# RMSNorm with ReLU on one core: 32-row blocks, joined stores, and VectorE's last two chunks taken whole

## The chip, the cores and the metric

One Trainium2 chip, one of its cores. The metric is the device time of one execution in microseconds.

## The reference, cut to what matters

```python
x = np.random.randn(16, 1024, 512).astype(np.float32)     # 16,384 rows of 512
gamma = np.ones(512, dtype=np.float32)
rms = np.sqrt(np.mean(x ** 2, axis=-1, keepdims=True) + 1e-5)
return np.maximum(x / rms * gamma, 0).astype(np.float32)
```

33.55 MB come in and 33.55 MB go out. Each row needs one sum of squares, one scale, one product with gamma and a maximum with 0.

## The kernel before

A partition owns 16 consecutive rows of each of 8 chunks, so a chunk is 4.19 MB and a packet of a transfer 32 KB. The kernel keeps six chunks in SBUF at a time. ScalarE sums the squares of 8 rows (a "group") and takes the roots; VectorE scales the group. SyncE issues all transfers and waits for two marks in VectorE's loop, `tick3` and `tick1`, before it lets stores go.

```python
xv = x2.rearrange("(c p k) d -> c p k d", p=P, k=K)       # K = 16
ov = out2.rearrange("(c p k) d -> c p k d", p=P, k=K)
# ... loads of chunks 0 to 5 are issued first (cut) ...
nc.sync.wait_ge(tick3, 6)
store(0)
store(1)
for s in range(2):
    nc.sync.wait_ge(sem_slot[s], 32)
    load(7 + s)                                           # chunks 6 and 7
nc.sync.wait_ge(tick1, 11)
for i in range(2, nchunks):
    store(i)
# ... (cut) ...
with nc.vector.Fori(0, ngroups) as gi:                    # 16 groups
    take(nc.vector, sq, 1)                                # wait and subtract
    # base, col, blk: addresses from gi (cut)
    nc.vector.reciprocal(out=rstd[...], in_=rms[...]).then_inc(sv, 1)
    take(nc.vector, sv, 1)
    for j in range(G):
        r = nc.vector.scalar_tensor_tensor(               # row * rstd * gamma
            out=row, in0=row, scalar=rstd[...], in1=gamma_sb, ...)
        # j == 0: tick1, j == 2: tick3, j == 7: sv
    take(nc.vector, sv, 1)
    nc.vector.tensor_scalar_max(out=blk, in0=blk, scalar1=0.0).then_inc(done, 1)
```

Of the kernel before, what the change touches and what calls it, by code (L numbers as in the profile page):

```python
# [1 line left out]

# [4 lines left out]

F32 = mybir.dt.float32
ALU = mybir.AluOpType
ACTF = mybir.ActivationFunctionType  # L10


@with_exitstack
def kernel(
    ctx: ExitStack,
    tc: tile.TileContext,
    x: bass.AP,
    gamma: bass.AP,
    eps: bass.AP,
    out: bass.AP,  # L20
):




    nc = tc.nc
    P = nc.NUM_PARTITIONS

    x2 = x.flatten_outer_dims()
    out2 = out.flatten_outer_dims()  # L30
    n, d = x2.shape
    rows = n // P
    inv_d = 1.0 / d
    K = 16
    G = 8
    nchunks = rows // K
    nslots = 6
    ngroups = rows // G
    per = K // G
    xv = x2.rearrange("(c p k) d -> c p k d", p=P, k=K)  # L40
    ov = out2.rearrange("(c p k) d -> c p k d", p=P, k=K)

    def sbuf(name, shape):
        return nc.alloc_sbuf_tensor(name, shape, F32).ap()

    gseed = sbuf("gseed", [P, d])
    gamma_sb = sbuf("gamma_sb", [P, d])
    eps_sb = sbuf("eps_sb", [P, 1])
    ss = sbuf("ss", [P, rows])
    rms = sbuf("rms", [P, rows])  # L50
    rstd = sbuf("rstd", [P, rows])
    slots = sbuf("slots", [P, nslots * K * d])
    junk = nc.alloc_psum_tensor("junk", [P, G, d], F32).ap()


    loads = [(0, 0, G), (0, G, K - G)] + [(i, 0, K) for i in range(1, nchunks)]


    sem_half = nc.alloc_semaphore("half")
    sem_slot = [nc.alloc_semaphore(f"slot{s}") for s in range(nslots)]  # L60
    sem_g = nc.alloc_semaphore("gam")
    sem_z = nc.alloc_semaphore("zero")
    ready = nc.alloc_semaphore("ready")
    sq = nc.alloc_semaphore("sq")
    tick1 = nc.alloc_semaphore("tick1")
    tick3 = nc.alloc_semaphore("tick3")
    done = nc.alloc_semaphore("done")
    sa = nc.alloc_semaphore("sa")
    sv = nc.alloc_semaphore("sv")

    def slot_ap(i):
        s = (i % nslots) * K * d
        return slots[:, s:s + K * d].rearrange("p (k d) -> p k d", d=d)

    def load(m):
        i, a, r = loads[m]
        return nc.sync.dma_start(out=slot_ap(i)[:, a:a + r, :],
                                 in_=xv[i][:, a:a + r, :]
                                 ).then_inc(sem_half if m == 0 else sem_slot[i % nslots], 16)

    def take(engine, sem, n):
        engine.wait_ge(sem, n)
        engine.sem_inc(sem, -n)  # L83

    def store(i):
        nc.sync.wait_ge(done, per * (i + 1))
        nc.sync.dma_start(out=ov[i], in_=slot_ap(i)).then_inc(sem_slot[i % nslots], 16)



    ctx.enter_context(tc.manual_schedule(engines={mybir.EngineType.SP}))
    early = 2
    for m in range(early):
        t = load(m)
        tc.no_tile_sem_insts.add(t.ins.name)
    ctx.close()
    tc.close()
    tc.compile()  # L98

    for m, (i, a, r) in enumerate(loads):  # L100
        if m >= early and i < nslots:
            load(m)


    nc.sync.wait_ge(tick3, 6)
    store(0)
    store(1)
    for s in range(2):
        nc.sync.wait_ge(sem_slot[s], 32)
        load(7 + s)  # L110
    nc.sync.wait_ge(tick1, 11)
    for i in range(2, nchunks):
        store(i)

    for m, (i, a, r) in enumerate(loads):
        if m == 0:
            take(nc.gpsimd, sem_half, 16)
        else:
            nc.gpsimd.wait_ge(sem_slot[i % nslots], 32 * (i // nslots) + 16)
        nc.gpsimd.sem_inc(ready, r // G)  # L120

    nc.vector.memset(gseed, 0.0).then_inc(sem_z, 1)  # L122
    nc.vector.memset(eps_sb, eps).then_inc(sem_z, 1)  # L123

    nc.scalar.wait_ge(sem_z, 1)
    nc.scalar.dma_start(out=gseed[0:P:32, :],
                        in_=gamma[None, :].to_broadcast([P // 32, d])
                        ).then_inc(sem_g, 16)
    nc.scalar.preload_act_table(ACTF.Sqrt)  # L129
    take(nc.scalar, sem_z, 2)  # L130
    with nc.scalar.Fori(0, ngroups) as gi:
        take(nc.scalar, ready, 1)
        base = nc.scalar.snap((gi % (nslots * per)) * (G * d))
        col = nc.scalar.snap(gi * G)
        for j in range(G):
            a = nc.scalar.activation(  # L136
                out=junk[:, j, :], in_=slots[:, bass.ds(base + j * d, d)],
                func=ACTF.Square, accum_out=ss[:, bass.ds(col + j, 1)])
            if j == G - 1:
                a.then_inc(sa, 1)  # L140
        take(nc.scalar, sa, 1)
        nc.scalar.activation(out=rms[:, bass.ds(col, G)], in_=ss[:, bass.ds(col, G)],  # L142
                             func=ACTF.Sqrt, bias=eps_sb, scale=inv_d).then_inc(sq, 1)

    take(nc.vector, sem_g, 16)
    nc.vector.stream_shuffle(gamma_sb, gseed, [0] * 32)  # L146
    with nc.vector.Fori(0, ngroups) as gi:
        take(nc.vector, sq, 1)
        base = nc.vector.snap((gi % (nslots * per)) * (G * d))
        col = nc.vector.snap(gi * G)  # L150
        blk = slots[:, bass.ds(base, G * d)]
        nc.vector.reciprocal(out=rstd[:, bass.ds(col, G)],  # L152
                             in_=rms[:, bass.ds(col, G)]).then_inc(sv, 1)
        take(nc.vector, sv, 1)
        for j in range(G):
            row = slots[:, bass.ds(base + j * d, d)]
            r = nc.vector.scalar_tensor_tensor(  # L157
                out=row, in0=row, scalar=rstd[:, bass.ds(col + j, 1)], in1=gamma_sb,
                op0=ALU.mult, op1=ALU.mult)
            if j == 0:  # L160
                r.then_inc(tick1, 1)
            if j == 2:
                r.then_inc(tick3, 1)
            if j == G - 1:
                r.then_inc(sv, 1)
        take(nc.vector, sv, 1)
        nc.vector.tensor_scalar_max(out=blk, in0=blk, scalar1=0.0).then_inc(done, 1)  # L167

    take(nc.sync, done, ngroups)
    take(nc.sync, tick1, ngroups)  # L170
    take(nc.sync, tick3, ngroups)
    for i in range(nchunks - nslots, nchunks):
        take(nc.sync, sem_slot[i % nslots], 32 * (i // nslots + 1))


# [1 line left out]
_INS = ['x', 'gamma', 'eps']  # L177
_OUTS = [((16, 1024, 512), 'float32')]

_NUMBERS = {'eps': 9.999999747378752e-06}  # L180


# [26 lines left out]
```

## Time and profile before

| | before |
|---|---|
| median of 3 runs (range) | 160.52 us (160.39 to 160.58) |
| span of the profiled run | 159.3 us |
| queue 1's share of the 16 DMA engines | 98.2% |
| VectorE busy, last instruction ends at | 126.0 us, 146.4 us |
| last store issued, landed (first to last of the 16 DMA engines) | 146.48, 157.66 to 158.74 us |

The rows of the page by group of instructions (line, engine, operation, operands, shape and count; then busy time and mean ns of one; then the idle time ahead of them and what ended it):

```profile
L157 DVE SCALAR_TENSOR_TENSOR slots<-slots,rstd,gamma_sb 128x512 f32 x128 | 86.2, 747 | 4.8 <-DVEq L83 4.8
L167 DVE TENSOR_SCALAR slots<-slots x16 | 36.7, 2294 | 2.4 <-DVEq L83 0.2
```

The 4.8 us of idle time ahead of 16 first products are 0.30 us each: a semaphore instruction and register work lie between the reciprocal and the product.

Besides the page I use the trace's records of single DMA packets. Each transfer ends, on each of the 16 DMA engines, in a 4-byte packet that puts up its semaphore; the times of these sixteen packets say when each engine is done with it. "First" and "last engine" below are the earliest and the latest of the sixteen.

### The profile page before, as it was taken

The page shows a single profiled execution, that of the slowest core. Times are in us where ns is not written, and L with a number is a line of the kernel's source. Part 1 is how long each engine was busy: PE and PEld are TensorE (multiplying, and loading weights), DVE is VectorE, ACT ScalarE, POOL GpSimd, SP SyncE. Part 2 cuts the span into 40 slices and gives each one's busy share as a digit, 9 for nine tenths or more (in the row PEclk, how much of TensorE's full clock was granted, in tenths as well). Part 3 has the DMA queues.
Part 4 walks back from the last instruction along what each step waited for, and adds up shares of the span by engine and source line. Part 5 has one row for each costly group of instructions (what it writes and reads, how often), then busy time and mean ns, then how long its engine had stood idle before and what let it go on. Part 6 is the DMA issues. An engine that isn't in the chain of part 4 may idle for free. (4 is left out here: it accounts for less than half of the span.)

```text
span 159.3 us, 999 instructions
## 1 busy us (share of the span) xinstructions
DVE 126.0 (79%) x164; ACT 86.3 (54%) x273; POOL 0.2 (0%) x4
## 2 busy tenths in 40 slices
DVE  1012989898999999999999999999999989897000
ACT  0388929889989988988920098898500000000000
POOL 0000000000000000000000000000000000000000
DMA  6999999999999999999999999999999999999995
GB/s 193 405 453 424 502 395 395 502 420 395 453 469 395 395 502 420 395 428 494 395 395 444 461 411 395 486 436 395 453 453 403 411 494 411 403 461 453 395 420 247
DMA packets 2456, 67.12 MB, mean 421 GB/s; under 512 B 276, under 2 KB 276, under 8 KB 280
## 3 DMA queue, kind: packets, MB, share of 16 engines
q1 hardware_dynamic: 2448, 67.11, 98.2%
q10 hardware_dynamic: 8, 0.01, 0.0%
HBM read 33.56 MB, written 33.55 MB: 421 GB/s over the span
## 5 line engine op out<-in xcount | busy, mean ns | idle before, releaser
L157 DVE SCALAR_TENSOR_TENSOR slots<-slots,rstd,gamma_sb 128x512 f32 x128 | 86.2, 747 | 4.8 <-DVEq L83 4.8
L136 ACT ACTIVATE junk<-slots 128x512 f32 x128 | 74.4, 581 | 20.6 <-ACTq L83 20.3
L167 DVE TENSOR_SCALAR slots<-slots x16 | 36.7, 2294 | 2.4 <-DVEq L83 0.2
L136 ACT ACTIVATION_READ_ACCUMULATOR junk<-slots x128 | 23.9, 187 | 0.0
L152 DVE RECIPROCAL rstd<-rms x16 | 3.1, 197 | 5.3 <-DVEq L83 5.3
L142 ACT ACTIVATE rms<-ss,eps_sb x16 | 4.8, 301 | 3.0 <-ACTq L83 3.0
L146 DVE LOAD_MASK_SELECT gamma_sb<-gseed x1 | 0.0, 14 | 5.4 <-DVEq L83 5.4
L129 ACT ACT_TABLE_LOAD x1 | 1.3, 1283 | 4.2 <-issue 4.2
L122 DVE MEMSET gseed<- 128x512 f32 x1 | 0.5, 485 | 2.6 <-PEq L98 2.6
L146 DVE STREAM_SHUFFLE gamma_sb<-gseed 128x512 f32<-128x512 f32 x1 | 0.7, 723 | 0.0
L190 POOL MEMSET const-bfloat16-1.0<- 128x1 bf16 x1 | 0.1, 102 | 0.0
L190 POOL MEMSET const-uint8-127<- 128x1 uint8 x1 | 0.1, 102 | 0.0
L190 POOL MEMSET const-float32-0.0<- 128x1 f32 x1 | 0.1, 99 | 0.2 <-issue 0.2
L190 POOL MEMSET const-float32-1.0<- 128x1 f32 x1 | 0.1, 99 | 0.0
L123 DVE MEMSET eps_sb<- 128x1 f32 x1 | 0.1, 59 | 0.0
## 6 DMA issues: line engine op xcount, KB each, us to landing
out_dram<-slots SPq DMA_DIRECT2D x8, 4096.0 KB, 20.6
slots<-in_x_dram SPq DMA_DIRECT2D x7, 4096.0 KB, 29.7
slots<-in_x_dram SPq DMA_DIRECT2D x2, 2048.0 KB, 9.7
gseed<-in_gamma_dram ACTq DMA_DIRECT2D x1, 8.0 KB
```

The source lines that it names most:

```text
L122: nc.vector.memset(gseed, 0.0).then_inc(sem_z, 1)
L123: nc.vector.memset(eps_sb, eps).then_inc(sem_z, 1)
L129: nc.scalar.preload_act_table(ACTF.Sqrt)
L136: a = nc.scalar.activation(out=junk[:, j, :], in_=slots[:, bass.ds(base + j * d, d)], func=ACTF.Square, accum_out=ss[:, bass.ds(col + j, 1)])
L142: nc.scalar.activation(out=rms[:, bass.ds(col, G)], in_=ss[:, bass.ds(col, G)], func=ACTF.Sqrt, bias=eps_sb, scale=inv_d).then_inc(sq, 1)
L146: nc.vector.stream_shuffle(gamma_sb, gseed, [0] * 32)
L152: nc.vector.reciprocal(out=rstd[:, bass.ds(col, G)], in_=rms[:, bass.ds(col, G)]).then_inc(sv, 1)
L157: r = nc.vector.scalar_tensor_tensor(out=row, in0=row, scalar=rstd[:, bass.ds(col + j, 1)], in1=gamma_sb, op0=ALU.mult, op1=ALU.mult)
L167: nc.vector.tensor_scalar_max(out=blk, in0=blk, scalar1=0.0).then_inc(done, 1)
L190: nc = _bacc.Bacc("TRN2", target_bir_lowering=False, num_devices=1)
```

## The change

The intent: fewer and larger store packets, fewer waits in VectorE's loop, and marks adapted to that.

1. In DRAM a partition owns 32 consecutive rows of chunks 2 and 3, and of 4 and 5. They are still loaded 16 rows at a time but leave in two joined stores with 64 KB packets.
2. Waits no longer subtract; the subtractions come at the end of the loop's body, and addresses are made before the wait.
3. One mark, on the sixth product, in place of two.
4. VectorE loops over 12 groups. Chunks 6 and 7 are taken whole, in two passes of 128 x 8192 each, the second one a custom operation (product and clamp).
5. The two small memsets move to GpSimd.

The core of the diff, with cuts marked:

```diff
+    order = [(L, 0, G), (L, G, G)] + [(L, i * K, K) for i in range(1, nslots)] + [
+        (S, 0, K), (S, K, K), (L, room, K), (L, room + K, K),
+        (S, 2 * K, 2 * K), (S, 4 * K, 2 * K), (S, room, K), (S, room + K, K)]
+    blocks = [(0, K), (K, K), (2 * K, 2 * K), (4 * K, 2 * K), (room, K), (room + K, K)]
 ... (cut)
+            if order[m - 1][0] == L:
+                nc.sync.wait_ge(tick, 6 if a == 0 else 11)
+            nc.sync.wait_ge(done, (a + r) // G)
 ... (cut)
-    with nc.vector.Fori(0, ngroups) as gi:
-        take(nc.vector, sq, 1)
+    with nc.vector.Fori(0, ndyn) as gi:          # ndyn = 12
 ... (cut)
-        take(nc.vector, sv, 1)
+        nc.vector.wait_ge(sv, 1)
         for j in range(G):
 ... (cut)
-            if j == 0:
-                r.then_inc(tick1, 1)
-            if j == 2:
-                r.then_inc(tick3, 1)
+            if j == G - 3:
+                r.then_inc(tick, 1)
 ... (cut)
+    for i in range(nslots, nchunks):
 ... (cut)
+        nc.vector.tensor_tensor(out=blk, in0=blk, in1=fac[:, :, None].to_broadcast([P, K, d]),
+                                op=ALU.mult).then_inc(sv, 1)
+        nc.vector.wait_ge(sv, steps + 2)
+        nc.vector._custom_dve(
+            dve_ops.TENSOR_MUL_SAT, out=blk, in0=blk,
+            in1=gamma_sb[:, None, :].to_broadcast([P, K, d]),
+            s0=float("inf"), s1=0.0).then_inc(done, per)
```

More of the change, by code (lines that the diff above doesn't have):

```diff
@@ L4 @@
 import concourse.tile as tile
-from concourse import bass_utils, mybir
+from concourse import bass_utils, dve_ops, mybir
 from concourse._compat import with_exitstack
@@ L39 @@
     per = K // G
-    xv = x2.rearrange("(c p k) d -> c p k d", p=P, k=K)
-    ov = out2.rearrange("(c p k) d -> c p k d", p=P, k=K)
     def sbuf(name, shape):
@@ L53 @@
     junk = nc.alloc_psum_tensor("junk", [P, G, d], F32).ap()
-    loads = [(0, 0, G), (0, G, K - G)] + [(i, 0, K) for i in range(1, nchunks)]
-    sem_half = nc.alloc_semaphore("half")
-    sem_slot = [nc.alloc_semaphore(f"slot{s}") for s in range(nslots)]
+    L, S = 0, 1
+    room = nslots * K
+    order = [(L, 0, G), (L, G, G)] + [(L, i * K, K) for i in range(1, nslots)] + [
+        (S, 0, K), (S, K, K), (L, room, K), (L, room + K, K),
+        (S, 2 * K, 2 * K), (S, 4 * K, 2 * K), (S, room, K), (S, room + K, K)]
+    blocks = [(0, K), (K, K), (2 * K, 2 * K), (4 * K, 2 * K), (room, K), (room + K, K)]
+    sems = [nc.alloc_semaphore(f"t{m}") for m in range(len(order))]
     sem_g = nc.alloc_semaphore("gam")
@@ L64 @@
     sq = nc.alloc_semaphore("sq")
-    tick1 = nc.alloc_semaphore("tick1")
-    tick3 = nc.alloc_semaphore("tick3")
+    tick = nc.alloc_semaphore("tick")
     done = nc.alloc_semaphore("done")
@@ L69, with here, transfer @@
     sv = nc.alloc_semaphore("sv")
-    def slot_ap(i):
-        s = (i % nslots) * K * d
-        return slots[:, s:s + K * d].rearrange("p (k d) -> p k d", d=d)
-    def load(m):
-        i, a, r = loads[m]
-        return nc.sync.dma_start(out=slot_ap(i)[:, a:a + r, :],
-                                 in_=xv[i][:, a:a + r, :]
-                                 ).then_inc(sem_half if m == 0 else sem_slot[i % nslots], 16)
+    def here(a, r):
+        a %= room
+        return slots[:, a * d:(a + r) * d].rearrange("p (k d) -> p k d", d=d)
+    def transfer(m):
+        kind, a, r = order[m]
+        first, k = max(b for b in blocks if b[0] <= a)
+        there = (out2 if kind == S else x2)[first * P:(first + k) * P].rearrange(
+            "(p k) d -> p k d", k=k)[:, a - first:a - first + r, :]
+        ends = (there, here(a, r)) if kind == S else (here(a, r), there)
+        return nc.sync.dma_start(out=ends[0], in_=ends[1]).then_inc(sems[m], 16)
     def take(engine, sem, n):
@@ L83, in take @@
         engine.sem_inc(sem, -n)
-    def store(i):
-        nc.sync.wait_ge(done, per * (i + 1))
-        nc.sync.dma_start(out=ov[i], in_=slot_ap(i)).then_inc(sem_slot[i % nslots], 16)
     ctx.enter_context(tc.manual_schedule(engines={mybir.EngineType.SP}))
@@ L93 @@
     for m in range(early):
-        t = load(m)
+        t = transfer(m)
         tc.no_tile_sem_insts.add(t.ins.name)
@@ L98 @@
     tc.compile()
-    for m, (i, a, r) in enumerate(loads):
-        if m >= early and i < nslots:
-            load(m)
-    nc.sync.wait_ge(tick3, 6)
-    store(0)
-    store(1)
-    for s in range(2):
-        nc.sync.wait_ge(sem_slot[s], 32)
-        load(7 + s)
-    nc.sync.wait_ge(tick1, 11)
-    for i in range(2, nchunks):
-        store(i)
-    for m, (i, a, r) in enumerate(loads):
-        if m == 0:
-            take(nc.gpsimd, sem_half, 16)
-        else:
-            nc.gpsimd.wait_ge(sem_slot[i % nslots], 32 * (i // nslots) + 16)
-        nc.gpsimd.sem_inc(ready, r // G)
-    nc.vector.memset(gseed, 0.0).then_inc(sem_z, 1)
-    nc.vector.memset(eps_sb, eps).then_inc(sem_z, 1)
+    for m, (kind, a, r) in enumerate(order):
+        if m < early:
+            continue
+        if kind == S:
+            if order[m - 1][0] == L:
+                nc.sync.wait_ge(tick, 6 if a == 0 else 11)
+            nc.sync.wait_ge(done, (a + r) // G)
+        elif a >= room:
+            take(nc.sync, sems[order.index((S, a - room, r))], 16)
+        transfer(m)
+    nc.gpsimd.memset(gseed, 0.0).then_inc(sem_z, 1)
+    nc.gpsimd.memset(eps_sb, eps).then_inc(sem_z, 1)
+    for m, (kind, a, r) in enumerate(order):
+        if kind == L:
+            take(nc.gpsimd, sems[m], 16)
+            nc.gpsimd.sem_inc(ready, r // G)
     nc.scalar.wait_ge(sem_z, 1)
@@ L131 @@
     with nc.scalar.Fori(0, ngroups) as gi:
-        take(nc.scalar, ready, 1)
         base = nc.scalar.snap((gi % (nslots * per)) * (G * d))
         col = nc.scalar.snap(gi * G)
+        nc.scalar.wait_ge(ready, 1)
         for j in range(G):
@@ L138 @@
                 func=ACTF.Square, accum_out=ss[:, bass.ds(col + j, 1)])
-            if j == G - 1:
-                a.then_inc(sa, 1)
-        take(nc.scalar, sa, 1)
+        a.then_inc(sa, 1)
+        nc.scalar.wait_ge(sa, 1)
         nc.scalar.activation(out=rms[:, bass.ds(col, G)], in_=ss[:, bass.ds(col, G)],
                              func=ACTF.Sqrt, bias=eps_sb, scale=inv_d).then_inc(sq, 1)
-    take(nc.vector, sem_g, 16)
+        nc.scalar.sem_inc(sa, -1)
+        nc.scalar.sem_inc(ready, -1)
+    nc.vector.wait_ge(sem_g, 16)
     nc.vector.stream_shuffle(gamma_sb, gseed, [0] * 32)
-    with nc.vector.Fori(0, ngroups) as gi:
-        take(nc.vector, sq, 1)
-        base = nc.vector.snap((gi % (nslots * per)) * (G * d))
+    ndyn = nslots * per
+    with nc.vector.Fori(0, ndyn) as gi:
+        base = nc.vector.snap(gi * (G * d))
         col = nc.vector.snap(gi * G)
         blk = slots[:, bass.ds(base, G * d)]
+        nc.vector.wait_ge(sq, 1)
         nc.vector.reciprocal(out=rstd[:, bass.ds(col, G)],
                              in_=rms[:, bass.ds(col, G)]).then_inc(sv, 1)
-        take(nc.vector, sv, 1)
+        nc.vector.wait_ge(sv, 1)
         for j in range(G):
@@ L159 @@
                 op0=ALU.mult, op1=ALU.mult)
-            if j == 0:
-                r.then_inc(tick1, 1)
-            if j == 2:
-                r.then_inc(tick3, 1)
-            if j == G - 1:
-                r.then_inc(sv, 1)
-        take(nc.vector, sv, 1)
-        nc.vector.tensor_scalar_max(out=blk, in0=blk, scalar1=0.0).then_inc(done, 1)
-    take(nc.sync, done, ngroups)
-    take(nc.sync, tick1, ngroups)
-    take(nc.sync, tick3, ngroups)
-    for i in range(nchunks - nslots, nchunks):
-        take(nc.sync, sem_slot[i % nslots], 32 * (i // nslots + 1))
+            if j == G - 3:
+                r.then_inc(tick, 1)
+        r.then_inc(sv, 1)
+        nc.vector.wait_ge(sv, 2)
+        nc.vector.tensor_scalar_max(out=blk, in0=blk, scalar1=0.0).then_inc(done, 1)
+        nc.vector.sem_inc(sv, -2)
+        nc.vector.sem_inc(sq, -1)
+    steps = 0
+    for i in range(nslots, nchunks):
+        blk = here(i * K, K)
+        fac = rstd[:, i * K:(i + 1) * K]
+        nc.vector.wait_ge(sq, per * (i - nslots + 1))
+        nc.vector.reciprocal(out=fac, in_=rms[:, i * K:(i + 1) * K]).then_inc(sv, 1)
+        nc.vector.wait_ge(sv, steps + 1)
+        nc.vector.tensor_tensor(out=blk, in0=blk, in1=fac[:, :, None].to_broadcast([P, K, d]),
[5 more added lines that the diff above has]
+            s0=float("inf"), s1=0.0).then_inc(done, per)
+        steps += 2
+    take(nc.sync, done, ngroups)
+    take(nc.sync, tick, ndyn)
+    take(nc.sync, sq, ngroups - ndyn)
+    take(nc.sync, sv, steps)
+    take(nc.sync, sem_g, 16)
+    for m, (kind, a, r) in enumerate(order):
+        if kind == S and a + room >= rows:
+            take(nc.sync, sems[m], 16)
 _INS = ['x', 'gamma', 'eps']
```

## The prediction

> **What bounds the kernel now.** The page comes first, its DMA rows before its engine rows.
>
> ```profile
> span 159.3 us, 999 instructions
> DVE 126.0 (79%) x164; ACT 86.3 (54%) x273; POOL 0.2 (0%) x4
> ...
> DMA  6999999999999999999999999999999999999995
> ...
> q1 hardware_dynamic: 2448, 67.11, 98.2%
> ...
> HBM read 33.56 MB, written 33.55 MB: 421 GB/s over the span
> ...
> DVE 1%; issue 0%
> ```
>
> The sixteen DMA engines are busy in every slice but the first and the last; queue 1 alone holds them 98.2% of 159.3, or 156.4 us. VectorE is busy 79% and has done its work before the end. The chain of waits, the last row, names almost nothing: the last instruction ends long before the span, so what ends last is a transfer, which the chain cannot follow. The bound is therefore DMA time plus the idle DMA at both ends.
>
> The second look is the timeline of the queue that issues the transfers, and of VectorE around its release points.
>
> ```profile
> 0.73 4.16 SPq L77 DMA_DIRECT2D slots<-in_x_dram  x7
> 58.30 0.82 SPq L87 DMA_DIRECT2D out_dram<-slots  x2
> 71.23 10.35 SPq L77 DMA_DIRECT2D slots<-in_x_dram  x2
> 98.19 48.62 SPq L87 DMA_DIRECT2D out_dram<-slots  x6
> ```
>
> ```profile
> 96.91 0.20 DVE L152 RECIPROCAL rstd<-rms  x1
> 97.41 5.39 DVE L157 SCALAR_TENSOR_TENSOR slots<-slots,rstd,gamma_sb 128x512 f32 x8 [0.30 <-DVEq L83]
> 102.95 2.29 DVE L167 TENSOR_SCALAR slots<-slots  x1
> ...
> 144.15 2.29 DVE L167 TENSOR_SCALAR slots<-slots  x1
> ```
>
> The first column is the start, the second the length. VectorE's group is eight row products, then one maximum; the reciprocals of two groups are 8.24 us apart. The first store starts at 58.30, exactly as the third row product of the sixth group ends (56.20 + 2 x 0.663 + 0.75 = 58.27); store 2 starts at 98.19, as the first row product of the eleventh group ends (97.41 + 0.75 = 98.16). So VectorE is no bound, but two marks in its loop set when the stores go out.
>
> The records of single DMA packets, third, show how little room the marks leave. Loads 0 to 5 put up their last semaphore packets at 60.68 to 61.05 us, load 7 at 99.57 to 100.08, the last store at 157.66 to 158.74. A transfer issued into an empty queue (the first, issued at 0.73) shows its first packet at 1.75, 1.02 us later. So the first store must be issued by about 59.6 and store 2 by about 98.5 (estimates: landing minus 1.02 us), or the engines run dry. Before, the margins are 1.3 and 0.3 us. The last store is issued at 146.48 for a queue that drains at 147.98: margin 0.5 us.
>
> **What the Trainium skill says.** "DMA: Bandwidth & Descriptors", section "Where 436 GB/s comes from", gives 435.2 GB/s for the ports of one core. The trace agrees: in steady loads 4.194 MB take 9.681 us, or 433 GB/s. At 435.2 the 67.11 MB would take 154.2 us; sixteen times 9.681 is 154.9. So faster packets can give at most 0.7 us altogether, an estimate from that page's figure.
>
> The same page, section "Why small descriptors are slow (HBM only)", tells of a fixed cost of about three cycles per packet. The trace agrees that it is tiny: packets of 16,384 B take 611 ns and of 32,768 B 1,213 ns, so 16 KB cost 602 ns and 9 ns are fixed (less still from one packet's start to the next, about 1,209 ns for 32 KB).
>
> "Perfetto Trace Analysis", section "Per-instruction lifecycle", has a VectorE instruction wait for its semaphores in a hardware queue while the sequencer goes on to decode. Before, every wait in VectorE's loop is a separate semaphore instruction that also subtracts: it runs 0.04 us after the producer ends, takes 21 ns, and the consumer starts only after more decoding. On the issuing queue, where a wait stands alone ahead of a transfer, the records show it inside the transfer's own instruction. I infer, and no run shows yet, that a wait without the subtraction will likewise be folded into the VectorE instruction behind it.
>
> "VectorE: DVE Perf Modes", section "The TRN2 errata", has fp32 tensor_tensor exact at (N + 151) / 0.96 ns. The trace has no such operation; for N = 8,192 the estimate from that page is 8.69 us.
>
> **The change, part by part.**
>
> Descriptors: a partition now owns 32 consecutive rows of chunks 2 to 5. Their loads still take 16 rows at a time, packets of 32 KB with a step of 64 KB. Their stores join in pairs: 4 x 128 = 512 packets of 32 KB become 256 of 64 KB. Per engine 16 packets vanish, of 136. At 5 to 9 ns each that is 0.08 to 0.14 us, plus two semaphore packets of 9 ns. Call it 0.1 us, on the path. The later issue of pairs costs nothing: done counts of 8 and 12 groups are reached at about 80 and 110 us, while their turns come at about 100 and 119.
>
> Waits in VectorE's loop: the gaps are 0.30 us between reciprocal and first row product and 0.16 between last product and maximum. With folded waits I expect them to shrink to about 0.08 and 0.06: 0.22 + 0.10 = 0.32 us a group. The gap ahead of the reciprocal is already hidden under the maximum. ScalarE's first group also starts earlier: 0.32 us lie between its released wait at 8.41 and its first square at 8.73, and 0.18 before the square root; with VectorE's own first wait, about 0.5 us. All this is off the path as long as DMA stays full. It moves the marks.
>
> Marks: both are now the sixth product. Unmoved, it would end at 56.20 + 5 x 0.663 + 0.75 = 60.26 in the sixth group and at 97.41 + 5 x 0.663 + 0.75 = 101.47 in the eleventh. Savings up to there: 0.5 + 6 x 0.22 + 5 x 0.10 = 2.3 us and 0.5 + 11 x 0.22 + 10 x 0.10 = 3.9 us. Issues then fall at 58.0 and 97.6 us, inside 59.6 and 98.5. No hole, no gain. That both results lie so near the old 58.3 and 98.2 speaks for a mark retuned to this faster loop.
>
> Tail of VectorE: twelve groups from about 14.0, at 8.24 - 0.32 = 7.92, end at 109.0. Each of the last chunks is two passes of 8.69 plus a reciprocal of 0.2 and waits of about 0.2: 17.8 us, against 16.5 for two groups before. The end is at 109.0 + 35.6 = 144.6, against 146.44 before. The last store is issued about 144.7, 2.3 us before its limit of 147.0. Store 6 is released at about 127, its turn comes at about 138. So this part is worth 0.
>
> Moving the memsets to GpSimd: gamma is needed at about 14 us, and before it had landed by 7.7. Worth 0.
>
> Sum: 160.52 - 0.1 = 160.4 us.
>
> **The rivals.**
>
> A: waits fold incompletely. Ahead of a row product the trace shows register work of 115 ns between wait and product. If the wait sits on that, only about 0.09 of the 0.30 us goes; store 2 is issued at 101.47 - (0.4 + 11 x 0.09 + 10 x 0.10) = 99.1, and the hole is 0.6 us: 161.0. If the product's wait stays a separate instruction, only the 0.10 is saved: 101.47 - 1.4 = 100.1, a hole of 1.6 us: 162.0. If nothing folds, 101.2 and 60.0 give holes of 2.7 and 0.4: 163.5. For it speaks that register work; against it that the edit puts waits directly ahead of instructions, which would make little sense otherwise, and that the two marks fit the full saving.
>
> B: the custom product-and-clamp runs at half rate. Then a pass takes 17.1 us instead of 8.7, VectorE ends near 161 and the last store near 173. Nothing in this trace shows the operation. Against it: it replaces a multiply and a clamp, an odd thing to do in a tuned kernel at half rate. There are 2.3 us of room, so only a rate below about 0.88 would be felt.
>
> C: the address step of 64 KB, or the larger packet, disturbs the transfers. One per cent on the 33.6 MB concerned is 0.8 us. For it speaks that the packets' durations already vary in stores (up to 1,713 ns). Against it, nearly all stand at 1,213 whatever the direction.
>
> D: the slowest DMA engine gains. The last of the sixteen finishes 1.08 us behind the first and falls behind mostly during stores, about 0.08 us per store. If the loss goes with packets or transfers, the joined stores save 0.2 to 0.3 more: 160.1.
>
> **Range and chances.** I give full folding 60%, with 160.1 to 160.6; rival A 30%, spread over 161.0, 162.0 and 163.5 with most on the first; B and C together 7%. The range is 159.9 to 161.6. Over 2% faster would be below 157.3, which needs 3.2 us where the packets can give 0.7 and the idle ends are untouched: 1%. Over 2% slower is above 163.8: the last case of A barely, or B: 4%. The rest, 95%, is within 2%.
>
> **What would show it.** Right: packets of 65,536 B at about 2,415 ns, queue 1 still about 98% busy, stores issued near 58.0 and 97.6, the gap before the first product under 0.15 us, VectorE done near 144.6. Wrong in A: the gap still 0.2 to 0.3, store 2 issued after 98.5, and a dip in the DMA row near 100 us. Wrong in B: a pass far over 8.7 us, and the last store issued after 147. Wrong in C: 32 KB packets of the middle loads above 1,213 ns, or a 64 KB packet clearly over twice that. A gain of over 0.7 us would mean that time at an end of the span, not packet time, was saved.

## The result, and the profile after

| | before | after |
|---|---|---|
| median of 4 runs (range) | 160.50 us (160.39 to 160.58) | 160.24 us (160.09 to 160.66) |
| ratio, 95% interval | | 0.9988 (0.9968 to 1.0008) |
| span of the profiled run | 159.3 us | 158.9 us |

A ratio is the mean time of one kernel's fast runs over that of the other's in the same rounds, so not quite the ratio of the medians quoted. On these four runs alone the gain is not clear of noise; the stand-in of the experiments settled that it is there.

The page after, the lines that answer those of before:

```profile
span 158.9 us, 902 instructions
DVE 129.4 (81%) x128; ACT 86.3 (54%) x273; POOL 0.8 (0%) x6
...
DMA  6999999999999999999999999996997998999996
...
q1 hardware_dynamic: 2160, 67.11, 98.3%
...
L153 DVE SCALAR_TENSOR_TENSOR slots<-slots,rstd,gamma_sb 128x512 f32 x96 | 64.7, 746 | 1.8 <-DVE rstd L148 1.8
...
L173 DVE CUSTOM_DVE_ANT_1 slots<-slots,gamma_sb 128x8192 f32<-128x8192 f32 x2 | 17.4, 8693 | 0.3
L170 DVE TENSOR_TENSOR slots<-slots,rstd 128x8192 f32<-128x8192 f32 x2 | 17.4, 8692 | 0.1
```

VectorE is busy longer (129.4 for 126.0 us) with fewer instructions (128 for 164), and DMA is as full as before. The 6 and 7 in the DMA row are no holes: a packet is counted in the slice in which it starts, and a 64 KB packet lasts 2.4 us of a slice of 4. The idle time ahead of the first products is down to 1.8 us for 12 groups, 0.15 each.

The timelines after, of the issuing queue and of VectorE (start, length, engine, line, operation):

```profile
0.73 4.04 SPq L82 DMA_DIRECT2D slots<-in_x_dram  x7
58.55 0.82 SPq L82 DMA_DIRECT2D out_dram<-slots  x2
71.38 10.26 SPq L82 DMA_DIRECT2D slots<-in_x_dram  x2
98.45 47.41 SPq L82 DMA_DIRECT2D out_dram<-slots  x4
```

```profile
94.01 0.20 DVE L148 RECIPROCAL rstd<-rms  x1
94.36 5.39 DVE L153 SCALAR_TENSOR_TENSOR slots<-slots,rstd,gamma_sb 128x512 f32 x8 [0.15 <-DVE rstd L148]
99.78 2.29 DVE L160 TENSOR_SCALAR slots<-slots  x1
102.00 0.19 DVE L148 RECIPROCAL rstd<-rms  x1
...
136.81 8.69 DVE L173 CUSTOM_DVE_ANT_1 slots<-slots,gamma_sb 128x8192 f32<-128x8192 f32 x1
```

The reciprocals are 7.98 us apart now, and both marks came out within 0.3 us of where they had been: stores at 58.55 and 98.45 against 58.30 and 98.19.

Where the time went can be read from the semaphore packets. Load 7 lands on its last engine at 100.08 before and at 100.09 after, so nothing had changed up to there. The last store lands on its last engine at 158.74 and 158.42. The whole 0.33 us lies in the last six stores. A single store of 32 KB packets takes 9.681 us at packet pace, a joined one of 64 KB packets 19.322: four stores in 38.64 instead of 38.72 us, 0.08 us. The remaining 0.25 us is not packet pace. One DMA engine, the one that ends last, lags behind the other fifteen while stores run: over the last six stores it loses 0.57 us before and 0.32 after. The loss is the time from load 7's last landing to the last store's last landing, less six stores at packet pace (58.09 us, or 58.01 with two joined). A trace of the packets engine by engine shows the same for before: one engine 0.60 us late over these stores, the other fifteen within 0.01. After, the engine that ends last loses 0.35 us when it is followed packet by packet; a second one loses 0.24, but it ends 0.39 us earlier and does not set the time.

### The profile page after: what moved, and what is told of

It is laid out like the page before. It is cut to its first block, busy times and chain, and to the rows that moved or that the text cites. A ratio compares the mean times of both kernels' runs of the same rounds, so it can differ in the third digit from the quotient of the medians.

```text
span 158.9 us, 902 instructions
## 1 busy us (share of the span) xinstructions
DVE 129.4 (81%) x128; ACT 86.3 (54%) x273; POOL 0.8 (0%) x6
## 3 DMA queue, kind: packets, MB, share of 16 engines
q1 hardware_dynamic: 2160, 67.11, 98.3%
## 4 chain that ended last, share of the span: by engine, by line
DVE 51%; issue 18%; DVEq 5%; ACT 3%; ACTq 0%; POOLq 0%
DVE slots L153 27%; DVE slots L170 11%; DVE slots L173 11%; DVEq L153 3%; ACT junk L130 3%; DVE rstd L148 1%; DVEq L143 1%; DVEq L148 0%; ACTq L130 0%; DVE rstd L168 0%; DVE slots L160 0%; ACT rms L135 0%; DVEq L162 0%; DVEq L172 0%; ACTq L135 0%
## 5 line engine op out<-in xcount | busy, mean ns | idle before, releaser
L153 DVE SCALAR_TENSOR_TENSOR slots<-slots,rstd,gamma_sb 128x512 f32 x96 | 64.7, 746 | 1.8 <-DVE rstd L148 1.8
L160 DVE TENSOR_SCALAR slots<-slots x12 | 27.5, 2294 | 0.4
L173 DVE CUSTOM_DVE_ANT_1 slots<-slots,gamma_sb 128x8192 f32<-128x8192 f32 x2 | 17.4, 8693 | 0.3
L170 DVE TENSOR_TENSOR slots<-slots,rstd 128x8192 f32<-128x8192 f32 x2 | 17.4, 8692 | 0.1
L148 DVE RECIPROCAL rstd<-rms x12 | 2.3, 195 | 5.4 <-ACT rms L135 5.4
L112 POOL MEMSET gseed<- 128x512 f32 x1 | 0.5, 525 | 1.9 <-POOLq L97 1.9
L168 DVE RECIPROCAL rstd<-rms 128x16 f32<-128x16 f32 x2 | 0.5, 246 | 0.0
```

Source lines behind the costliest of these rows:

```text
L112: nc.gpsimd.memset(gseed, 0.0).then_inc(sem_z, 1)
L148: nc.vector.reciprocal(out=rstd[:, bass.ds(col, G)], in_=rms[:, bass.ds(col, G)]).then_inc(sv, 1)
L153: r = nc.vector.scalar_tensor_tensor(out=row, in0=row, scalar=rstd[:, bass.ds(col + j, 1)], in1=gamma_sb, op0=ALU.mult, op1=ALU.mult)
L168: nc.vector.reciprocal(out=fac, in_=rms[:, i * K:(i + 1) * K]).then_inc(sv, 1)
L170: nc.vector.tensor_tensor(out=blk, in0=blk, in1=fac[:, :, None].to_broadcast([P, K, d]), op=ALU.mult).then_inc(sv, 1)
L173: nc.vector._custom_dve(dve_ops.TENSOR_MUL_SAT, out=blk, in0=blk, in1=gamma_sb[:, None, :].to_broadcast([P, K, d]), s0=float("inf"), s1=0. ...
```

## The experiments

Two theories of the remaining 0.25 us. **P**: the loss goes with packets or transfers, so joining the stores halves it (the prediction's rival D). **I**: it goes with the number of small instructions that the engines execute while stores run, and the whole passes removed VectorE's loop from that stretch.

The base is a stand-in with a standard operation of the same shape, equal here because gamma is all ones.

### The stand-in, twice

```diff
-        nc.vector._custom_dve(
-            dve_ops.TENSOR_MUL_SAT, out=blk, in0=blk,
-            in1=gamma_sb[:, None, :].to_broadcast([P, K, d]),
-            s0=float("inf"), s1=0.0).then_inc(done, per)
+        nc.vector.scalar_tensor_tensor(
+            out=blk, in0=blk, scalar=0.0, in1=gamma_sb[:, None, :].to_broadcast([P, K, d]),
+            op0=ALU.max, op1=ALU.mult).then_inc(done, per)
```

> The changed kernel with its custom product-and-clamp replaced by a standard operation of the same shape, maximum with 0 and then product with gamma (equal here, gamma is all ones); it is the base of further experiments. Both theories: the pass takes 8.69 us as the custom one did, VectorE ends at about 145.5, store 2 is issued at 98.45, and the time is that of the changed kernel, 160.1 to 160.4. If the standard operation were slower than about 9.4 us a pass, the last store would be late and the time longer.

> The stand-in kernel once more, as the partner of the next run on the same chip. 0.3 to 0.4 us below the kernel before of the same rounds, about 120 instructions and a loss of 0.33 us on the last engine over the last six stores.

Measured: 160.29 us against 160.68 of before, ratio 0.9973 (0.9959 to 0.9986), and 160.31 against 160.81, ratio 0.9967 (0.9954 to 0.9981). The pass is as long as the custom one:

```profile
L173 DVE SCALAR_TENSOR_TENSOR slots<-slots,gamma_sb 128x8192 f32<-128x8192 f32 x2 | 17.4, 8692 | 0.2
```

The loss over the last six stores is 0.33 us in both profiled runs, as in the changed kernel. So the stand-in stands for it, and it is 0.3% faster than before, clear of noise. The first prediction for the time held. The gain over before by the medians, 0.39 us and 0.50, was larger than the traces' 0.33, and the second larger than the 0.3 to 0.4 that I had expected. The kernel before had medians of 160.5 to 160.95 us. Kernels are compared only within the same rounds. All outputs are right.

### The blocks and joined stores alone, and everything but them

Kernel before with the layout of chunks 2 to 5 and two joined stores, all else as before:

```diff
+    def dram(t, i):
+        if 2 <= i < 6:
+            j = i // 2 * 2
+            return t[j * K * P:(j + 2) * K * P].rearrange(
+                "(p k) d -> p k d", k=2 * K)[:, (i - j) * K:(i - j + 1) * K, :]
+        return t[i * K * P:(i + 1) * K * P].rearrange("(p k) d -> p k d", k=K)
 ... (cut: used for loads and stores)
-    for i in range(2, nchunks):
-        store(i)
+    store2(2)
+    store2(4)
+    store(6)
+    store(7)
```

> The kernel before with the 32-row blocks and the two joined stores alone; loop, waits and marks as before. Theory P (packets and joined stores give the gain): the four stores of chunks 2 to 5 take 0.08 us less on every engine and the last DMA engine lags less in them (0.3 us rather than 0.5), so the whole gain is here: 160.1 to 160.3. Theory I (the last engine lags because of the many small instructions that run during the stores, and the whole-chunk tail removes those of VectorE): only the 0.08 us of the packets is here, the last engine still ends 1.0 us behind the first: 160.4 to 160.45.

The stand-in with single stores again:

```diff
-        (S, 2 * K, 2 * K), (S, 4 * K, 2 * K), (S, room, K), ...
+        (S, 2 * K, K), (S, 3 * K, K), (S, 4 * K, K), (S, 5 * K, K), (S, room, K), ...
-    blocks = [..., (2 * K, 2 * K), (4 * K, 2 * K), ...]
+    blocks = [..., (2 * K, K), (3 * K, K), (4 * K, K), (5 * K, K), ...]
```

> The stand-in kernel with chunks 2 to 5 back in 16-row blocks and four single stores of 32 KB packets; loop, waits, marks and whole-chunk tail as changed. Theory P: 0.08 us of packet time and the lag come back, 160.4 to 160.5. Theory I: only the packet time comes back, the last engine still ends about 0.8 us behind the first, 160.25 to 160.35.

Measured: blocks alone 160.51 us, ratio to before 0.9988 (0.9974 to 1.0001); single stores 160.42 us, ratio 0.9983 (0.9969 to 0.9996). Of the packets, both show the 0.08 us: two joined stores in 38.64 us on the first engine with blocks alone, four single ones in 38.73 with single stores. Of the loss, theory P falls: with joined stores and the old loop it is 0.60 us, as large as before; with single stores and whole passes it is 0.33, as small as after. Both times lie above what theory I gave: 160.42 for 160.25 to 160.35 with single stores, 160.51 for 160.40 to 160.45 with blocks alone; the medians differ by tenths for which five runs are few, and I rest the verdict on the packet records. The times do not contradict it: no run of blocks alone (160.38 to 160.59) was as fast as the slowest of the stand-in's five (160.33).

### The loop kept to the end

```diff
-    ndyn = nslots * per
+    ndyn = ngroups
-        base = nc.vector.snap(gi * (G * d))
+        base = nc.vector.snap((gi % (nslots * per)) * (G * d))
-    for i in range(nslots, nchunks):
- ... (cut: the two whole chunks)
```

> The changed kernel with VectorE's loop over all 16 groups instead of the two whole chunks; blocks, joined stores, waits and marks as changed. VectorE should end about 14.2 + 16 x 7.98 = 141.9, earlier than the changed kernel's 145.5, which is worth nothing to the end. Theory P: 160.2, the last engine 0.8 us behind the first as in the changed kernel. Theory I: the lag grows again by 0.2 to 0.3 us between 115 and 142 us, 160.4 to 160.5.

Measured: 160.47 us, ratio 0.9991 (0.9977 to 1.0004), loss 0.55 us: theory I. VectorE's last maximum, here and in the stand-in's last pass (start, length):

```profile
140.34 2.29 DVE L160 TENSOR_SCALAR slots<-slots  x1
```

```profile
136.94 8.69 DVE L173 SCALAR_TENSOR_TENSOR slots<-slots,gamma_sb 128x8192 f32<-128x8192 f32 x1
```

VectorE ends 3 us earlier with the loop, at 142.6 against 145.6, and the kernel ends later. It had slack in either case. One blemish: the remainder in the address makes the loop 0.05 us a group slower, store 2 goes out at 98.86, past its limit (98.5 by the prediction, 98.52 to 98.66 by the late-mark run below), and the first engine takes 0.23 us longer over it. The last engine, busy until 100.18, does not notice.

### Small instructions on an idle engine

```diff
+    with nc.gpsimd.Fori(0, 70) as pi:            # after GpSimd's last wait
+        for j in range(2):
+            nc.gpsimd.sem_inc(spare, 1)
+            nc.gpsimd.sem_inc(spare, -1)
```

> The stand-in kernel with a loop on GpSimd after its last wait: 70 rounds of four additions to a spare semaphore and the loop's own instructions, some 500 small instructions between about 101 and 140 us, no data moved. Theory I (small instructions on any engine slow one DMA engine): VectorE's loop in the tail cost the last engine 0.22 to 0.27 us with about 110 instructions more than the whole passes have, some 2 ns each, so 500 make about 1.1 us: the last engine falls about 1.4 us behind over the last six stores instead of 0.33, time about 161.4. Theory V (it is VectorE's own row operations and their reads, not instructions as such): the loss over the last six stores stays at 0.33 and the time at 160.3.

Measured: 161.69 us against 160.95 of before, ratio 1.0051 (1.0034 to 1.0067), slower clear of noise. The page:

```profile
span 160.4 us, 1323 instructions
DVE 129.4 (81%) x128; ACT 86.3 (54%) x273; POOL 0.8 (0%) x6
```

The engines do the same work, and 421 instructions more are executed than in the stand-in, none of which moves data. The loss over the last six stores is 1.64 us. It sits on one engine: its 64 KB packets between 100 and 138 us take 2,498 to 2,573 ns, where nearly all others take 2,418; the next latest engine is 0.23 us late over these stores, all others within 0.04. After 138.5 us, when the loop has ended, its packets are back at pace. This decides between VectorE's operations and instructions as such: theory I, at (1.64 - 0.33) / 421 = 3.1 ns per instruction. Of the 421, 280 are semaphore additions and 141 the loop's register work and branches; no run parts the two kinds.

### ScalarE's last two groups with fixed addresses

```diff
-    with nc.scalar.Fori(0, ngroups) as gi:
+    nloop = ngroups - 2
+    with nc.scalar.Fori(0, nloop) as gi:
 ... (cut: the same body, then once more for groups 14 and 15 with numbers for addresses)
```

> The stand-in kernel with ScalarE's last two groups, which run from about 102 to 114 us beside the first joined store, written out with fixed addresses: the same 16 squares and 2 roots, without the register work and the branch. In the stand-in the last engine loses 0.28 of its 0.33 us there. Theory I: a third to a half of the instructions in that stretch go, the loss falls to 0.15 to 0.2 us, 160.1 to 160.2. Theory W (ScalarE's squares themselves, their reads, slow the engine): the loss stays 0.28 and the time 160.3.

Measured: 160.36 us, ratio to before 0.9965 (0.9951 to 0.9979), loss 0.25 us. I had expected a third to a half of the instructions to go; the page counts 876 for 902, so only 26 went, and 26 x 3 ns is the 0.08 us that the loss fell by. The squares stayed, so theory W, which wanted no change, is not what is seen, though the step is small. The time is above the 160.1 to 160.2 that I had given, with the kernel before at 160.95.

The runs that part the theories, in one table. Instructions are those executed between load 7's last landing and the last store's last landing, on all engines:

| kernel | stores 2 to 5 | VectorE's tail | instructions | loss, us | ns each |
|---|---|---|---|---|---|
| before | single | loop | 218 | 0.57 | 2.6 |
| blocks alone | joined | loop | 218 | 0.60 | 2.7 |
| loop kept | joined | loop | 211 | 0.55 | 2.6 |
| after | joined | whole | 120 | 0.32 | 2.7 |
| stand-in | joined | whole | 122 | 0.33 | 2.7 |
| single stores | single | whole | 121 | 0.33 | 2.7 |
| ScalarE fixed | joined | whole | 93 | 0.25 | 2.7 |
| GpSimd's loop | joined | whole | 541 | 1.64 | 3.0 |

Packet size and number of transfers do not matter to the loss; the count of instructions does. The table compares last landing with last landing, which follows one engine only if the same one is last both times. In the run without marks, told below, it is not: 118 instructions go with a loss of 0.05 by this reckoning, but followed packet by packet one engine loses about 0.3 us there too, and another engine was last at load 7. While only loads run the loss is not seen: in the stand-in 340 instructions run from 20 to 60 us, and there first and last engine take the same 9.68 to 9.72 us per load; the engine that later loses, followed packet by packet, falls at most 0.06 us behind.

### Fewer instructions in every stretch with stores

ScalarE's groups 8 to 15 and VectorE's groups 6 to 11 written out in the same way:

```diff
-    with nc.scalar.Fori(0, ngroups) as gi:
+    nloop = 8
+    with nc.scalar.Fori(0, nloop) as gi:
 ... (cut: groups 8 to 15 with numbers for addresses)
-    with nc.vector.Fori(0, ndyn) as gi:
+    nvec = 6
+    with nc.vector.Fori(0, nvec) as gi:
 ... (cut: groups 6 to 11 with numbers for addresses)
```

> The stand-in kernel with ScalarE's groups 8 to 15 and VectorE's groups 6 to 11 written out with fixed addresses: the same operations on data, no register work, no branches, no subtractions in the stretches where stores run. Theory I, at the 2.7 ns per instruction that the runs so far give: instructions from 61 to 81 us fall from 174 to about 85 and in the last 58 us from 122 to about 75, worth 0.2 and 0.1 us on the engine that ends last: 0.2 to 0.35 us below the stand-in of the same rounds, and below both kernels of the study. If the loss has a floor or belongs to the operations on data, no difference over 0.1 us.

Measured: 160.32 us, ratio to before 0.9964 (0.9950 to 0.9978), the same as the stand-in's 160.31 in those rounds. My expectation failed. The instructions had gone as expected, 85 from 61 to 81 us and about 71 in the last stretch. The engine that ends last here loses nothing over the last six stores (58.005 us for 58.006), but it is another engine, which had fallen behind earlier. The one that theory I is about, followed packet by packet, loses 0.23 us, 3.2 ns for each of the 71. The DMA part of the page has a line that the stand-in's lacks:

```profile
q1 hardware_dynamic: 2160, 67.11, 98.3%
q14 instruction: 2, 0.02, 0.0%
```

The written-out program is longer and fetches two blocks of 8 KB while it runs, at 60.98 and 75.45 us, 309 ns each. On the engine that ends last the packet after 75.45 starts 117 ns late and takes 1,672 ns instead of 1,213. I infer that the second fetch ran on this engine; the records do not name engines. The kernel with ScalarE fixed shows the same once: it has one such fetch, at 114.30 us, and one engine's packet starts 0.2 us late just then and takes 2,651 ns instead of 2,418; that engine was not the last, and the fetch cost no time. So the gain was given back to another late engine, and this version beats before but not the changed one.

### The marks: too late and none

Mark late:

```diff
-            if j == G - 3:
+            if j == 0:
-                nc.sync.wait_ge(tick, 6 if a == 0 else 11)
+                nc.sync.wait_ge(tick, 6 if a == 0 else 12)
```

> The stand-in kernel with the mark on the first product, waiting for the sixth and the twelfth group: the first store goes out earlier than needed, at about 55.5, the second at about 103.3 us, 4.7 us later than in the stand-in. By the prediction's margin (the limit is the landing less 1.02 us) the DMA engines stand still from 100.1 to 104.3 us: about 4.2 us longer on the last engine, 164.3 to 164.9. Rival: a store into an empty queue starts within 0.3 us of its issue, then 163.6.

Marks taken out:

```diff
-            if order[m - 1][0] == L:
-                nc.sync.wait_ge(tick, 6 if a == 0 else 11)
```

> The stand-in kernel without the two marks: stores are issued as soon as their groups are done, store 0 at about 30 us, store 2 right after load 7 at about 82. If the queue of each DMA engine runs in order, early issue changes nothing: 160.2 to 160.4, loads land as before, and the marks only had to be early enough. Rival: an early store shares the engines with the loads queued before it, loads land later, ScalarE and VectorE start later, and the time is over 161.

Late, one look: 164.24 us. The issue and the hole (second fence: start and end; length, busy time of VectorE, ScalarE, GpSimd with counts; clock; DMA share; GB/s):

```profile
103.28 42.69 SPq L82 DMA_DIRECT2D out_dram<-slots  x4
```

```profile
96.00:100.00 4.00, 3.97 (x7) 3.52 (x13) 0.00 (x0) 1.00 0.91 393
100.00:104.00 4.00, 3.85 (x5) 3.52 (x13) 0.00 (x0) 1.00 0.00 0
104.00:108.00 4.00, 3.97 (x7) 4.00 (x14) 0.00 (x0) 1.00 1.22 524
```

Here is what a missed mark looks like: not a packet of data starts between 100 and 104 us while VectorE and ScalarE are busy. The first packet comes at 104.12, 0.84 us after the issue, and the last engine's first at 104.26, 0.98 after, where I had taken 1.02 from the first load. On the last engine the hole is 3.4 us, from load 7's landing at 100.70 to 104.12; load 7 itself landed 0.6 us later than in the stand-in, which the first mark, early in this kernel, explains below. Together that is the 3.9 us of the time. In the changed kernel load 7 lands on its first engine at 99.50, so the limit for store 2 lies between 99.50 - 0.98 = 98.52 and 99.50 - 0.84 = 98.66 us, and its 98.45 is 0.1 to 0.2 us inside. A few engines do show gaps of up to 0.06 us ahead of store 2 there, the one that ends last none.

Without marks: 160.68 us, ratio to before 0.9991 (0.9972 to 1.0011). The stand-in had 0.9973 and 0.9967; the timing alone does not part them, but the records show what is lost. With store 0 issued at 30.18 us, load 5 lands on its last engine 10.55 us after load 4, instead of 9.71, and the last two packets of the load on each engine take up to 1,968 ns, where the changed kernel's take 1,224 at most. In the late-mark kernel, whose first store goes out at 55.40, load 5 takes 10.42. So the first mark has a limit on the early side too, somewhere between 55.4 and 58.3 us; why a waiting store slows the end of the loads ahead of it stays open. The expected "changes nothing" was wrong. The second mark shows little of the kind: store 2 went out at 82.42 and load 7 took 9.81, for 9.72 in the stand-in.

### All transfers in 4 KB packets

```diff
+        there = (out2 if kind == S else x2)[first * P:(first + k) * P].rearrange(
+            "(h p q) d -> p h q d", p=P, q=2)[:, (a - first) // 2:(a - first + r) // 2]
+        mine = here(a, r).rearrange("p (h q) d -> p h q d", q=2)
+        ends = (there, mine) if kind == S else (mine, there)
```

> The stand-in kernel with every transfer cut into pieces of 2 rows, 4 KB packets: 1,024 packets of data per engine instead of about 120. At the 5 to 9 ns per packet of the prediction that is 900 x 5 to 9 ns = 4.5 to 8.1 us more: 165 to 168.5, a packet of 4 KB at about 160 ns. If the cost of a packet were nearer the 0 that would make 64 KB packets worth nothing, 160.5; if it were tens of ns, over 178.

Measured in one look: 167.06 us. Against the stand-in's 160.31 that is 6.75 us for some 900 packets per engine, 7.5 ns a packet, within the 5 to 9 of the prediction. So 16 packets saved per engine are worth 0.1 us, and the 0.08 seen fits. It is one look, and the order of addresses changed with the packets; but it gives no sign of a large packet cost that bigger packets could still save.

## Why the prediction was right, point by point

The time of 160.24 us fell in the range, 0.16 below the 160.4 given, and "within 2%" was right. That alone says little of the mechanism: a gain of 0.1 us, as reckoned, and one of 0.33, as the traces show, both lie in a range of 1.7 us. The larger part of the gain came from a part that the prediction had called worth 0, and that the total came so near is in this respect luck.

**The bound.** Right: DMA is the bound before and after (98.2% and 98.3%), and what the change moved was tenths of a us at DMA's own end.

**Descriptors.** Right in mechanism and size: 64 KB packets took 2,418 ns, 0.08 us were saved at packet pace, predicted 0.08 to 0.14, and the 4 KB run agrees with the cost per packet.

**Waits.** Right in direction, mis-sized in three terms. The gap ahead of the first product became 0.15, not 0.08 us, because the wait sat on the register instruction ahead of the product, as rival A had feared; that instruction also became shorter, 65 for 115 ns. The gap ahead of the maximum became 0.03 where 0.06 was given. The group became 0.26 us shorter, for 0.32, and the head start was 0.27 us, for 0.5.

**Marks.** So the eleventh group's mark came at 98.45, for 97.6, and the first at 58.55, for 58.0. Both are within the limits, the second barely within the one I had stated (98.5). A hole as in rival A's milder case did not come, beyond the gaps of up to 0.06 us told above.

**VectorE's tail.** The passes are right: 8.69 us, the custom one as well, so rival B fell. The end came at 145.5, for 144.6. "So this part is worth 0" is the step that failed. It reckoned VectorE's time alone, which indeed was off the path. What counted was that the whole passes replace some 100 small instructions in the stretch of the stores, and at 2.7 ns each that gave the last DMA engine 0.25 us in these traced runs. This is the larger part of the gain.

**The rivals.** A and C did not happen: 32 KB packets stayed at 1,213 ns with a step of 64 KB. D had the right place, the last engine, the right size, 0.2 to 0.3 us, and the wrong cause: with joined stores alone the loss stayed at 0.60 us. Its 0.08 us per store was read a little low: over the last six it is 0.60 / 6 = 0.10.

What stays open is why one DMA engine pays for instructions. All runs here, timed ones too, list spans and clocks from a trace, so I cannot say whether writing the instruction records is itself that load. In that case a run without a trace would gain only the 0.08 us.

## What to carry to other kernels

When DMA is full from end to end, ask which of the sixteen engines ends last and what else it has to do: in these traced runs an engine well off the path cost time through the number of its instructions, not through their duration. A mark that releases a transfer has a window: the second one 4.6 us late left a hole of 3.4 us, and the first one 3 us early cost 0.7 us at the end of the loads. And before taking many small steps out of a loop by writing it out, look for instruction fetches in the DMA part of the page.

## What the Trainium skill lacked or had wrong

- No page has it: while stores run, one DMA engine loses about 2.7 to 3 ns for each instruction executed on VectorE, ScalarE or GpSimd (0.25 us at 93 instructions, 1.64 at 541); while only loads run this is not seen. Whether it is there in runs without a trace is open.
- "DMA: Bandwidth & Descriptors", section "Where 436 GB/s comes from", says that for transfers between HBM and SBUF the HBM side, about 358 GB/s, binds. Here one core moved 433 GB/s in steady loads (4.194 MB in 9.681 us), near the page's 435.2 for the ports. The sentence lacks its condition: the figure is a share of two cores, and the same page's own measurement for one core alone, 425 GB/s, agrees with what is seen here.
- The same page lacks what a store queued behind loads costs: the load ahead of it ended 0.7 to 0.8 us later when the store was issued at 55.4 us or before, and not when it was issued at 58.3 to 58.7.
- "VectorE: DVE Perf Modes", section "The TRN2 errata", holds beyond the sizes it names: (8,192 + 151) / 0.96 = 8,691 ns, measured 8,692. No page has the custom product-and-clamp by name: 8,693 ns, as long as the built-in operation.
- "Perfetto Trace Analysis", section "Per-instruction lifecycle", has the wait with the VectorE instruction. What it lacks: where the instruction has register work of its own ahead of it (the first product), the record shows the wait on that register instruction, and 0.15 us remain between reciprocal and product. Where it has none (the maximum, and the whole pass with its fixed address), the wait is the instruction's own and 0.03 us remain.
